# Group softmax: tiles of 256 rows with two adjacent rows per partition, on one queue

## The chip, the cores and the metric

One core of one Trainium2 chip runs the kernel. The metric is the device time of one execution in microseconds, the slowest core's, here the only one's.

## The reference

```python
def reference(x):                       # x: 4 x 4096 x 4352, float32
    x_g = x.reshape(B, N, 8, D // 8)    # 8 groups of 544 in a row
    x_g = x_g - x_g.max(axis=-1, keepdims=True)
    exp = np.exp(x_g)
    out = exp / exp.sum(axis=-1, keepdims=True)
    return out.reshape(B, N, D).astype(np.float32)
```

There are 16,384 rows of 17,408 bytes. Every byte is read once and written once: 285.2 MB each way.

## The kernel before

A tile is 128 rows, one per partition. Loads and stores go out on one queue. Per tile, VectorE (DVE) takes the eight maxima, ScalarE (ACT) does eight exponentials that also sum, and DVE does one reciprocal and eight scalings, in place.

```python
NBUF = 12
pool = ctx.enter_context(tc.tile_pool(name="io", bufs=NBUF))
xg = xf.rearrange("n (g d) -> n g d", g=G)
nt = N // P                                            # 128 tiles
def load(i):
    xt = pool.tile([P, G, Dg], f32, name="xt")         # 17 KB per partition
    nc.sync.dma_start(out=xt, in_=xg[i * P:(i + 1) * P])
# ... store, expo (max and 8 exponentials), scale (reciprocal and 8 scalings)
AHEAD = NBUF - 2
for i in range(AHEAD):
    load(i)
for i in range(nt + 1):
    if i < nt:
        expo(i)
    if i:
        scale(i - 1)
        store(i - 1, nc.sync)
        if i - 1 + AHEAD < nt:
            load(i - 1 + AHEAD)
```

## Time and profile before

| | before |
|---|---|
| time, median of the first 3 runs | 1342.13 us (1341.66 to 1342.44) |
| span of the profiled run | 1340.1 us |
| moved by the 16 DMA engines | 429 to 432 GB/s in mid kernel |
| DVE busy, ACT busy | 78%, 57% |
| store waits ahead of a load, in the queue | 116 waits, 1104.5 us |

Read it from the rate down. The rate is flat, no compute engine is full, and the queue spends its time waiting for stores to land before it reuses their buffers. The prediction shows the lines.

Two kinds of figure below come from the trace's own records and not from a line of a view. The first is the record of each packet on a DMA engine: start, duration, bytes. The second is the 16 landings of each transfer, one per DMA engine (before: 4,096 for 256 transfers). "Lag" means how much later the slowest engine lands its share of a transfer than the median engine. "Row" means one contiguous piece moved between memory and one partition, which is one packet (before: 32,768 packets of 17,408 B, and 4,096 of 4 B that end a transfer on an engine). "Steady" means the median engine's time for one transfer in mid kernel. A "ring" is the list of transfers that one DMA engine still has to do. SP is the engine whose sequencer (SPq in the views) issues the transfers of the queue.

### The profile page before, as it was taken

The page shows a single profiled execution, that of the slowest core. Times are in us where ns is not written, and L with a number is a line of the kernel's source. Part 1 is how long each engine was busy: PE and PEld are TensorE (multiplying, and loading weights), DVE is VectorE, ACT ScalarE, POOL GpSimd, SP SyncE. Part 2 cuts the span into 40 slices and gives each one's busy share as a digit, 9 for nine tenths or more (in the row PEclk, how much of TensorE's full clock was granted, in tenths as well). Part 3 has the DMA queues.
Part 4 walks back from the last instruction along what each step waited for, and adds up shares of the span by engine and source line. Part 5 has one row for each costly group of instructions (what it writes and reads, how often), then busy time and mean ns, then how long its engine had stood idle before and what let it go on. Part 6 is the DMA issues. An engine that isn't in the chain of part 4 may idle for free.

```text
span 1340.1 us, 4119 instructions
## 1 busy us (share of the span) xinstructions
DVE 1046.7 (78%) x1280; ACT 764.3 (57%) x2049; POOL 0.2 (0%) x4
## 2 busy tenths in 40 slices
DVE  6999987878777887888777877778877887777760
ACT  5777766555655565556555556555665556555540
POOL 0000000000000000000000000000000000000000
DMA  9999999999999999999999999999999999999996
GB/s 399 426 429 431 430 430 432 432 432 431 431 432 430 432 431 432 431 431 431 431 430 431 432 430 432 431 430 431 431 432 430 432 431 429 430 431 431 430 432 266
DMA packets 36896, 570.70 MB, mean 426 GB/s; under 512 B 4096, under 2 KB 4096, under 8 KB 4096
## 3 DMA queue, kind: packets, MB, share of 16 engines
q1 hardware_dynamic: 36864, 570.44, 99.4%
q14 instruction: 32, 0.26, 0.0%
HBM read 285.21 MB, written 285.21 MB: 426 GB/s over the span
## 4 chain that ended last, share of the span: by engine, by line
DMA 88%; DVE 7%; SPq 1%; ACT 1%; issue 1%; DVEq 0%; ACTq 0%
DMA out_dram<-xt 85%; DVE mx L45 4%; DVE xt L63 3%; DMA xt<-in_x_dram 3%; SPq L37 1%; ACT xt L49 1%; DVE rs L61 0%; DVEq L104 0%; ACTq L104 0%
## 5 line engine op out<-in xcount | busy, mean ns | idle before, releaser
L49 ACT ACTIVATE xt<-xt,mx 128x544 f32<-128x544 f32 x1024 | 751.2, 735 | 524.3 <-issue 435.8
L45 DVE TENSOR_REDUCE mx<-xt 128x8 f32<-128x4352 f32 x128 | 599.6, 4685 | 247.6 <-DMA xt<-in_x_dram 247.6
L63 DVE TENSOR_SCALAR xt<-xt,rs 128x544 f32<-128x544 f32 x1024 | 434.2, 498 | 4.5
L49 ACT ACTIVATION_READ_ACCUMULATOR xt<-xt,mx 128x1 f32 x1024 | 191.3, 187 | 0.0
L61 DVE RECIPROCAL rs<-sm 128x8 f32<-128x8 f32 x128 | 24.7, 193 | 3.4 <-ACT xt L49 3.4
L49 ACT ACT_TABLE_LOAD x1 | 1.3, 1283 | 9.9 <-DMA xt<-in_x_dram 9.9
L93 POOL MEMSET const-bfloat16-1.0<- 128x1 bf16 x1 | 0.1, 101 | 0.0
L93 POOL MEMSET const-uint8-127<- 128x1 uint8 x1 | 0.1, 101 | 0.0
L93 POOL MEMSET const-float32-0.0<- 128x1 f32 x1 | 0.1, 98 | 0.2 <-issue 0.2
L93 POOL MEMSET const-float32-1.0<- 128x1 f32 x1 | 0.1, 98 | 0.0
## 6 DMA issues: line engine op xcount, KB each, us to landing
xt<-in_x_dram SPq DMA_DIRECT2D x128, 2176.0 KB, 25.8
out_dram<-xt SPq DMA_DIRECT2D x128, 2176.0 KB, 30.6
```

Of the source, the lines that this page charges most:

```text
L37: nc.sync.dma_start(out=xt, in_=xg[i * P:(i + 1) * P])
L45: nc.vector.reduce_max(out=mx, in_=xt, axis=mybir.AxisListType.X, negate=True)
L49: nc.scalar.activation(out=xt[:, g, :], in_=xt[:, g, :], func=mybir.ActivationFunctionType.Exp, bias=mx[:, g:g + 1], scale=1.0, accum_out= ...
L61: nc.vector.reciprocal(out=rs, in_=sums.pop(i))
L63: nc.vector.tensor_scalar_mul(out=xt[:, g, :], in0=xt[:, g, :], scalar1=rs[:, g:g + 1])
L93: nc = _bacc.Bacc("TRN2", target_bir_lowering=False, num_devices=1)
```

## The change

The intent is fewer and longer transfers with the same buffer space: two adjacent rows per partition make one contiguous row of 34 KB, 128 transfers take the place of 256, and the queue alternates store i and load i+5. The kept core of the diff:

```diff
-    NBUF = 12
+    R = 2
+    NBUF = 6
...
+    def rows(dram, i):
+        at, r = spans[i]
+        return dram[at:at + r * P].rearrange("(p r) d -> p (r d)", r=r)
+
     def load(i):
-        xt = pool.tile([P, G, Dg], f32, name="xt")
+        xt = pool.tile([P, R * D], f32, name="xt")
         tiles[i] = xt
-        nc.sync.dma_start(out=xt, in_=xg[i * P:(i + 1) * P])
+        nc.sync.dma_start(out=xt[:, :spans[i][1] * D], in_=rows(xf, i))
...
-    AHEAD = NBUF - 2
+    AHEAD = NBUF - 1
+    work = [(i, r) for i in range(nt) for r in range(spans[i][1])]
...
+        for n in range(len(work) + 1):
+            if n < len(work):
+                expo(*work[n])
+            if n:
+                i, r = work[n - 1]
+                scale(i, r)
+                if r == spans[i][1] - 1:
+                    store(i)
+                    if i + AHEAD < nt:
+                        load(i + AHEAD)
```

`expo` and `scale` do to row r of tile i what they did to a tile, with the same instructions.

More of the change, by code (lines that the diff above doesn't have):

```diff
@@ L23, with store, row, expo @@
     Dg = D // G
-    xg = xf.rearrange("n (g d) -> n g d", g=G)
-    og = of.rearrange("n (g d) -> n g d", g=G)
-    nt = N // P
+    f32 = mybir.dt.float32
     pool = ctx.enter_context(tc.tile_pool(name="io", bufs=NBUF))
     small = ctx.enter_context(tc.tile_pool(name="small", bufs=4))
-    f32 = mybir.dt.float32
+    spans = []
+    at = 0
+    while at < N:
+        r = min(R, (N - at) // P)
+        spans.append((at, r))
+        at += r * P
+    nt = len(spans)
     tiles = {}
     sums = {}
+    def rows(dram, i):
+        at, r = spans[i]
+        return dram[at:at + r * P].rearrange("(p r) d -> p (r d)", r=r)
     def load(i):
-        xt = pool.tile([P, G, Dg], f32, name="xt")
+        xt = pool.tile([P, R * D], f32, name="xt")
         tiles[i] = xt
-        nc.sync.dma_start(out=xt, in_=xg[i * P:(i + 1) * P])
-    def store(i, eng):
-        eng.dma_start(out=og[i * P:(i + 1) * P], in_=tiles.pop(i))
-    def expo(i):
-        xt = tiles[i]
+        nc.sync.dma_start(out=xt[:, :spans[i][1] * D], in_=rows(xf, i))
+    def store(i):
+        nc.sync.dma_start(out=rows(of, i), in_=tiles[i][:, :spans[i][1] * D])
+    def row(i, r):
+        return tiles[i][:, r * D:(r + 1) * D].rearrange("p (g d) -> p g d", g=G)
+    def expo(i, r):
+        xr = row(i, r)
         mx = small.tile([P, G], f32, name="mx")
-        nc.vector.reduce_max(out=mx, in_=xt, axis=mybir.AxisListType.X, negate=True)
+        nc.vector.reduce_max(out=mx, in_=xr, axis=mybir.AxisListType.X, negate=True)
         sm = small.tile([P, G], f32, name="sm")
-        sums[i] = sm
+        sums[i, r] = sm
         for g in range(G):
             nc.scalar.activation(
-                out=xt[:, g, :],
-                in_=xt[:, g, :],
+                out=xr[:, g, :],
+                in_=xr[:, g, :],
                 func=mybir.ActivationFunctionType.Exp,
@@ L56, in expo, with scale @@
             )
-    def scale(i):
-        xt = tiles[i]
+    def scale(i, r):
+        xr = row(i, r)
         rs = small.tile([P, G], f32, name="rs")
-        nc.vector.reciprocal(out=rs, in_=sums.pop(i))
+        nc.vector.reciprocal(out=rs, in_=sums.pop((i, r)))
         for g in range(G):
-            nc.vector.tensor_scalar_mul(out=xt[:, g, :], in0=xt[:, g, :], scalar1=rs[:, g:g + 1])
-    AHEAD = NBUF - 2
+            nc.vector.tensor_scalar_mul(
+                out=xr[:, g, :], in0=xr[:, g, :], scalar1=rs[:, g:g + 1])
+    AHEAD = NBUF - 1
+    work = [(i, r) for i in range(nt) for r in range(spans[i][1])]
     with tc.manual_schedule():
@@ L70 @@
             load(i)
-        for i in range(nt + 1):
-            if i < nt:
-                expo(i)
-            if i:
-                scale(i - 1)
-                store(i - 1, nc.sync)
-                if i - 1 + AHEAD < nt:
-                    load(i - 1 + AHEAD)
+        for n in range(len(work) + 1):
[8 more added lines that the diff above has]
+                        load(i + AHEAD)
 _INS = ['x']
```

## The prediction

> **What bounds the kernel now.** I read the page first, for busy shares and the rate of the transfers.
>
> ```profile
> span 1340.1 us, 4119 instructions
> DVE 1046.7 (78%) x1280; ACT 764.3 (57%) x2049; POOL 0.2 (0%) x4
> ...
> GB/s 399 426 429 431 430 430 432 432 432 431 431 432 430 432 431 432 431 431 431 431 430 431 432 430 432 431 430 431 431 432 430 432 431 429 430 431 431 430 432 266
> ...
> q1 hardware_dynamic: 36864, 570.44, 99.4%
> HBM read 285.21 MB, written 285.21 MB: 426 GB/s over the span
> ```
>
> DVE and ACT have room; the 16 DMA engines are busy for 99.4% of the span and move 430 to 432 GB/s in every slice but the first two and the last. Then the queue's own waits and its timeline, to see what holds the queue back:
>
> ```profile
> SPq L37 <- DMA out_dram<-xt: 1104.5, 116, 16.7
> ```
>
> ```profile
> 105.00 0.33 SPq L37 DMA_DIRECT2D xt<-in_x_dram  x1
> 105.38 0.81 SPq L40 DMA_DIRECT2D out_dram<-xt  x1
> 115.38 0.33 SPq L37 DMA_DIRECT2D xt<-in_x_dram  x1
> 115.76 0.79 SPq L40 DMA_DIRECT2D out_dram<-xt  x1
> ```
>
> 116 loads wait for a store that has to free their buffer, and as soon as one goes out the next store follows 0.4 us later: the result was ready long before. One load and one store take 10.3 us, which is 4.456 MB at 431 GB/s. The chain of waits agrees, 85% of it stores and nothing else for a thousand us. DVE's 247.6 us of waiting for loads is the other face of it: compute runs up to the newest tile and then stands. Last, the tail, by stretches (columns: stretch, its us, busy us of DVE, ACT, POOL, clock, DMA share, GB/s):
>
> ```profile
> 1310.00:1320.00 10.00, 0.00 (x0) 0.00 (x0) 0.00 (x0) 1.00 1.00 428
> 1320.00:1325.00 5.00, 0.00 (x0) 0.00 (x0) 0.00 (x0) 1.00 0.97 414
> 1325.00:1330.00 5.00, 0.00 (x0) 0.00 (x0) 0.00 (x0) 1.00 0.24 101
> 1330.00:1335.00 5.00, 0.00 (x0) 0.00 (x0) 0.00 (x0) 1.00 0.19 80
> 1335.00:1340.10 5.10, 0.00 (x0) 0.00 (x0) 0.00 (x0) 1.00 0.08 34
> ```
>
> Twelve or thirteen DMA engines are through at about 1325.5 us. Three work on alone (0.19 of 16 is 3), the last until 1339.3. The landings of each store on the 16 engines show it building up: the slowest engine is 1.6 us behind the median at the first load, 6.2 us behind half way and 13.8 us at the end. So **the bound is the slowest DMA engine, which never stands idle**; everything else waits for it.
>
> [...]
> [...] In the tail, where single engines can be followed packet by packet, each row has a record of 648 ns and the next starts 644 to 645 ns after it[...]. The 4-byte packet that ends each transfer on an engine shifts the next by 6 ns (its record is 9 ns).
> [...] 12 tiles of 17 KiB and 6 of 34 KiB are both 204 KiB[...].
>
> **The change part by part.**
> (1) Descriptors. 256 transfers with 8 rows per engine become 128 with 8 rows of 34,816 B. [...] One engine before: 256 x (8 x 644.7 + 6 ns) = 1321.9 us; the undisturbed engines in fact take from 1.8 to 1325.5, 1323.7 us. After: 128 x (8 x 1284.7 + 6 ns) = 1316.3 us. Saved: **5.6 us**, 4.8 of it from 1024 rows fewer per engine at 4.7 ns and 0.8 from 128 end packets at 6 ns. It falls on the slowest engine too, so it is on the path in full.
> (2) The slow engines' lag. The trace has 32 instruction fetches of 8 KB on a queue of their own; each occupies one engine for about 309 ns, and the next row there has a record lengthened by 100 to 530 ns. DVE and ACT keep exactly the same instructions (1280 and 2049), only the queue's sequencer has 128 transfers fewer. So I leave the 13.8 us as they are, with some 3 us either way: change **0**.
> (3) Queue depth. Before, a load waits for the store three earlier; when it is released, two loads and two stores of 5.16 us are still in the rings, 20.6 us. After, load i+5 waits for store i-1, with load i+4 and store i behind it: 2 x 10.3, again 20.6 us. The lag of 14 us fits within that in both, so the fast engines do not run dry either, and the slowest certainly not. Change **0**.
> (4) Compute. Per two rows of each partition DVE has 2 x (4.69 + 0.19 + 3.39) = 16.5 us, ACT 2 x 5.9 = 11.8, against 20.6 us of transfer. The one new delay: the second row of tile i is scaled only after the first maximum of tile i+1, so store i can go some 4.7 + 3.6 = 8.3 us after load i+1 landed. It is wanted 31 us after that landing (store i-3, load i+2, store i-2 come between, at 10.3 each). Margin 22 us where it was about 48. Change **0**.
> (5) Ends. The first load lands about 5.2 us later (10.3 instead of 5.16 of transfer), so DVE starts at 15 instead of 9.9 and store 0 is ready at about 37 us. But five loads keep the rings full until about 54 us, as ten did. At the end the last load is followed by five stores, 51.6 us, as by ten before; the last tile needs about 4.7 + 2 x 5.9 + 4.7 = 22 us and its store is wanted after 41. Change **0**.
> Sum: 1342.1 - 5.6 = **1336.5 us**, 0.4% faster.
>
> **Rivals.**
> *Fixed cost is not per row.* If the long row is cut into pieces of the old size, or if the gap of 4.7 ns comes with bytes and not with rows, only the end packets go: 1342.1 - 0.8 = 1341.3. For it: before there is one row size only, so the trace cannot show the split by itself[...]. One chance in seven.
> *The rows of one tile get coupled.* If the order between instructions is kept for the whole tile and not for the row touched, the second maximum has to wait for the first row's exponentials, and the first scaling for the second row's. A tile then costs DVE 4.69 + 5.9 + 4.69 + 5.9 + 3.6 = 24.8 us, more than 20.6; 64 of them are 1587 us, and with ends about 1600, 19% slower. Nothing in the trace before can show it, since there a tile had one maximum and one scaling. The rows are separate column ranges, so I give it one chance in twenty or less.
> *A coarser pipeline starves.* Fewer, bigger pieces could leave the rings empty when something is late by over 20 us. The longest waits in the trace are 4.6 us (ACT, for nothing shown) and 9.9 (DVE, first load); margins of 20 and 22 us take them. If one in ten of the 64 turns lost 2 us, it would be 13 us more, 1349.
> *The lag changes.* [...] if the fetches spread differently, 3 us either way.
>
> **Range and chances.** Centre 1336.5. The cut-row rival and a lag larger by 3 us reach 1341; a lag smaller by 3 to 4 us, or rows with even less overhead, reach 1332. The runs before spread over 0.8 us only. Range 1332 to 1341.5. Over 2% faster would be below 1315[...]: 0.01. Over 2% slower needs the coupling or a real starvation: 0.05. Within 2%: 0.94.
>
> **What will show it.** Packets about 18,432 on the queue, with 16,384 rows; a row's record near 1288 ns, and 1285 from start to start. The rate in mid slices at 433 instead of 431. Loads waiting for stores on the queue still, about 58 of them, and one load plus one store every 20.57 us. Tail: most engines done near 1320, the last some 13 us later. DVE and ACT busy times unchanged. Wrong would be: rows still of 648 ns; the queue waiting for DVE's scaling in mid kernel; ACT or DVE waiting for each other within a tile at each turn; a slice below 425 GB/s.

Passages are cut where marked; no term of the sum is: 1342.1 - 5.6 = 1336.5 us, with 1284.7 ns for the long row and 4.7 ns for each row fewer. Before the change, with one row size, the trace gave only the 644.7 ns from start to start (mean of 112 on the engine that ends last; 650 to 651 across an end packet, so 6 ns for it), and the other two were the assumption. The records after have 1284.7 ns there (mean of 105), and 2 x 644.7 - 1284.7 is 4.7 ns.

## The result, and the profile after

| | before | after |
|---|---|---|
| time, median of 4 runs | 1342.04 us | 1335.57 us (1334.61 to 1336.10) |
| span of the profiled run | 1340.1 us | 1333.5 us |
| ratio | | 0.9951, 95% interval 0.9934 to 0.9968 |

Ratios here and below are the mean time of one kernel's runs over that of the other's of the same rounds, so they are not quite the ratio of the medians quoted. Executions over 1.5% slower than the fastest of the same kernel are left out of the means. The kernel is faster, clear of noise, by half a per cent; at the 2% threshold it is the same.

The page after has the lines that answer to those of before:

```profile
span 1333.5 us, 3809 instructions
DVE 1041.7 (78%) x1280; ACT 764.4 (57%) x2049; POOL 0.2 (0%) x4
...
GB/s 403 428 423 432 432 432 431 433 432 431 432 432 434 434 432 434 430 434 434 434 431 433 434 434 434 431 432 435 432 434 432 431 434 434 433 435 433 433 433 283
...
q1 hardware_dynamic: 18432, 570.43, 99.3%
q14 instruction: 28, 0.23, 0.0%
```

The packets have halved to 18,432. DVE and ACT do the same work. The rate in mid kernel is some 2 GB/s higher, but the third slice is not: 423 in place of 429.

The queue's own waits and two turns of its timeline (start, duration, instruction):

```profile
SPq L47 <- DMA out_dram<-xt: 1145.0, 58, 20.7
SPq L50 <- DVE xt L76: 91.2, 7, 22.5
```

```profile
87.39 0.33 SPq L47 DMA_DIRECT2D xt<-in_x_dram  x1
87.81 0.38 SPq L50 DMA_DIRECT2D out_dram<-xt  x1
108.66 0.33 SPq L47 DMA_DIRECT2D xt<-in_x_dram  x1
109.04 0.42 SPq L50 DMA_DIRECT2D out_dram<-xt  x1
```

The wait is the same one: 58 loads, each for a store that frees its buffer, with the next store ready 0.4 us later. Of the seven waits for the scaling, four (40.1 us) lie before 200 us, where compute catches up, and three (51.1 us) after 1250 us, at the last stores; none lies between. The DMA share is 0.97 or more in every stretch from 5 to 1320 us, so they cost next to nothing. The tail by stretches (us, busy us of DVE, ACT and POOL, clock, DMA share, GB/s):

```profile
1310.00:1320.00 10.00, 0.00 (x0) 0.00 (x0) 0.00 (x0) 1.00 0.98 425
1320.00:1325.00 5.00, 0.00 (x0) 0.00 (x0) 0.00 (x0) 1.00 0.29 125
1325.00:1330.00 5.00, 0.00 (x0) 0.00 (x0) 0.00 (x0) 1.00 0.13 56
1330.00:1333.50 3.50, 0.00 (x0) 0.00 (x0) 0.00 (x0) 1.00 0.05 20
```

Most engines finish just after 1320 us. Two (0.13 of 16 is 2) work on to 1332. So the end still belongs to the slowest DMA engine.

The 6.6 us between the two profiled spans split up as follows.

| | before | after | difference |
|---|---|---|---|
| 256 rows loaded and stored, steady | 20.652 us | 20.563 us | -0.089 us; 64 times: -5.7 us |
| last landing, median engine | 1325.4 us | 1320.9 us | -4.5 us |
| lag of the slowest engine at the last store | 13.9 us | 11.7 us | -2.2 us |

The steady rate gains 5.7 us, the start gives 1.1 us of it back, and a smaller lag adds 2.2 us. The start is visible in the stretches of 40 to 60 and 60 to 100 us, first before, then after:

```profile
40.00:60.00 20.00, 19.93 (x23) 14.86 (x41) 0.00 (x0) 1.00 1.01 425
60.00:100.00 40.00, 39.82 (x51) 29.81 (x80) 0.00 (x0) 1.00 1.00 430
```

```profile
40.00:60.00 20.00, 19.89 (x29) 14.84 (x40) 0.00 (x0) 1.00 0.99 409
60.00:100.00 40.00, 39.82 (x50) 29.16 (x81) 0.00 (x0) 1.00 1.00 427
```

409 in place of 425 GB/s for 20 us is 0.8 us, 427 in place of 430 for 40 us is 0.3 us. Such stretches count whole rows, so their edges are rough, but the landings agree: how far they run ahead of those before, followed back from mid kernel to the start along a straight line, gives 1.05 us lost here and 0.6 us in the repetition below. The DMA share is 0.99, so no ring is empty there; the last two rows of the fifth load, just ahead of the first store, are longer, and this load lands 11.1 us after the fourth in place of 10.3. Rows starting between 50 and 60 us carry 13.4 us above their normal length after (28 of them by over 20 ns), 5.0 us before (17). Why they are longer was not tried.

### The profile page after: what moved, and what is told of

It is laid out like the page before. It is cut to its first block, busy times and chain, and to the rows that moved or that the text cites. A ratio compares the mean times of both kernels' runs of the same rounds, so it can differ in the third digit from the quotient of the medians.

```text
span 1333.5 us, 3809 instructions
## 1 busy us (share of the span) xinstructions
DVE 1041.7 (78%) x1280; ACT 764.4 (57%) x2049; POOL 0.2 (0%) x4
## 4 chain that ended last, share of the span: by engine, by line
DMA 92%; DVE 4%; ACT 1%; SPq 1%; issue 0%; DVEq 0%; ACTq 0%
DMA out_dram<-xt 89%; DMA xt<-in_x_dram 3%; DVE mx L58 2%; DVE xt L76 1%; ACT xt L62 1%; SPq L47 1%; DVE rs L74 0%; DVEq L121 0%; ACTq L121 0%; ACTq L62 0%; SPq L50 0%
```

## The experiments

Theory A is the prediction's: each DMA engine pays a fixed cost of about 4.7 ns per row and 6 ns for the packet that ends a transfer, whatever the length, and the slowest engine sets the end. (From start to start in the last transfers, 17,408 B took 644.7 ns before and 34,816 B took 1284.7 after: two short rows cost 4.7 ns more than a long one. The end packet shifts the next row by 6 ns in both.) Rival B: the gain is from the number of transfers, the queue's turns or their order. Rival C: it is a smaller lag, by luck. Eleven kernels were run. The first four ran together on one chip, the next four together, and the last three together, each with its own runs of the kernel before (medians 1342.10, 1342.49 and 1341.54 us; single runs from 1339.59 to 1343.53).

### The change again

The edit is none.

> The changed kernel once more, beside the three others on one chip. Theory A (a fixed cost of about 4.7 ns per row and 6 ns per end packet on every DMA engine) and every rival: 1335.6 us within 1 us, ratio 0.995. It gives the noise of the lag: if the last DMA engine's lag differs by more than 2 us from the 11.7 us of the first run, part of the 6.5 us is luck.

Measured: 1336.38 us (1335.29 to 1336.96), ratio 0.9960 (0.9947 to 0.9972). Steady: 10,282.3 ns for a transfer, 10,281.5 the first time. Lag at the end: 12.9 us, where it was 11.7. The steady part repeats to a nanosecond; the lag differs by a microsecond between the two profiles, and the times of single runs by up to 2.4 us.

### The same transfers with rows of 17 KB

```diff
-        return dram[at:at + r * P].rearrange("(p r) d -> p (r d)", r=r)
+        return dram[at:at + r * P].rearrange("(r p) d -> p r d", r=r)
```

(The tile side of both transfers is viewed as `p r d` to match.)

> The changed kernel with its tiles, its buffers, its queue order and its 128 transfers, but with row p and row p+128 in partition p, so that each transfer has 256 rows of 17 KB again. Theory A: 1024 more rows per engine at 4.7 ns, 4.8 us, give 1340.4 us (ratio to before 0.9988), packet records of 648 ns. Rival B (the gain is from the halved number of transfers, end packets and queue turns, or from the new queue order): 1335.6 us. Rival C (the gain is a smaller lag by luck): either.

Measured: 1339.09 us (1338.35 to 1339.27), ratio 0.9979 (0.9967 to 0.9992). The page has twice the data packets:

```profile
q1 hardware_dynamic: 34816, 570.43, 99.6%
```

Its time lies between the two theories' numbers, so the total alone does not decide. The landings do. Steady, a transfer takes 10,320.3 ns here and 10,282.3 with long rows: 38 ns, times 128 is 4.9 us, against 4.8 expected by theory A and 0 by B. Against the kernel before (2 x 5,163.0 ns) it is 5.7 ns per transfer less: the one end packet that is saved, predicted as 6. So both terms of the sum hold, and **the row length is what the steady gain comes from**. What moves the total off 1340.4 is the lag: 11.4 us in this profile, 12.9 us in the one above, 13.9 us in the profile before.

### Rows of 52 KB

```diff
-    R = 2
-    NBUF = 6
+    R = 3
+    NBUF = 4
```

> The changed kernel with three adjacent rows per partition, four buffers and 86 transfers: rows of 52 KB. Theory A: 336 rows fewer per engine at 4.7 ns and 42 end packets fewer at 6 ns, 1.8 us less than the changed kernel: 1333.8 us, packet records near 1928 ns. Rival (a coarser pipeline starves): store i is now ready 8 us after load i+1 landed, and the rings have about 31 us of work behind a freed buffer, so no loss is expected in mid kernel, but if a margin is missed it is 1340 us or more and the queue waits for the scaling. Rival (long rows are cut): records of at most 34 KB lengths and 1335 to 1340 us.

Measured: 1336.49 us (1335.99 to 1337.77), ratio 0.9962 (0.9950 to 0.9975). The expected 1.8 us did not come. The rows are not cut: 10,752 packets of 52,224 B with records of 1,928 ns, and steadily 15,404.7 ns for a transfer, where theory A has 8 x 1924.7 + 6 = 15,403.6 (1284.7 ns and another 640.0 for 17,408 B more). The rings ran dry at the start:

```profile
40.00:60.00 20.00, 19.93 (x26) 15.61 (x43) 0.00 (x0) 1.00 0.87 376
60.00:100.00 40.00, 39.83 (x51) 29.18 (x79) 0.00 (x0) 1.00 1.01 417
```

In the queue's timeline load 3 goes out at 50.21 us, behind store 0, while its buffer was free from the beginning and the three first loads (46 us of transfer) are through. So my check of the margins had covered mid kernel and not the start.

### Rows of 52 KB, all four buffers loaded at the start

```diff
-        for i in range(AHEAD):
+        for i in range(NBUF):
             load(i)
...
-                    if i + AHEAD < nt:
+                    if NBUF <= i + AHEAD < nt:
```

> The kernel of e3_rows52 with its fourth buffer loaded at the start, where e3 issued load 3 only behind store 0, at 50.2 us, when the first three loads were nearly through; e3 moved 376 GB/s between 40 and 60 us. Theory (rows of 52 KB cost 1.8 us less per engine than rows of 34 KB, and e3 lost some 4 us of that and more to rings that ran dry in its first 100 us): 1332 to 1333 us. Rival (the long rows themselves bring nothing more): 1336 us as the changed kernel, with no gap at 40 to 60 us.

Measured: 1333.49 us (1333.20 to 1334.45), ratio 0.9944 (0.9931 to 0.9958). The stretch of 40 to 60 us of this kernel:

```profile
40.00:60.00 20.00, 19.93 (x26) 15.60 (x43) 0.00 (x0) 1.00 0.98 423
```

One extra load at the start is worth about 3 us (2.4 by the ratios, each to its own kernel before), and it uncovers the gain of the longer rows, which in the steady part is 17.6 ns for 384 rows loaded or stored, 1.5 us over the run. Its median is 2.9 us under that of the changed kernel and 2.1 us under the first measurement. It was run at another time. It beats the kernel before; that it beats the changed kernel too is not shown, since the two ratios' intervals overlap.

### Rows cut into pieces of 2,176 B

```diff
-        xt = pool.tile([P, G, Dg], f32, name="xt")
+        xt = pool.tile([P, G, Dg + 4], f32, name="xt")[:, :, :Dg]
```

> The kernel before with 16 unused bytes behind each group in the tile, so that each row of 17 KB becomes 8 pieces of 2,176 B; same tiles, transfers, order and compute. Theory A: 14,336 more pieces per engine (256 transfers x 56) at 4.7 ns, 67 us: 1409 us, ratio 1.050, starts of pieces about 84.7 ns apart. If the gap came with bytes and not with pieces: 1342 us.[...]

Measured: 1444.45 us (1444.37 to 1444.48), ratio 1.0766. A miss: the direction and the kind are right, but theory A's 67 us are 102. Steady, a transfer takes 5,583.2 ns, so a piece takes 87.1 ns and not 84.7. In the last transfer the starts are these:

```
start to start, ns:  85  90  84  90  84  90  85  89  85  89
```

The mean of 87.1 is two values in turn. One is the 84.7 ns of theory A, the other, 89 to 90 ns, about 5 ns more. So in this store every second piece, of equal length, is slower; why was not shown. At the start, where only loads run, a transfer takes 5,650 to 5,760 ns, which theory A does not cover either. The next run tests whether the excess goes away.

### Rows cut into pieces of 4,352 B

```diff
-        xt = pool.tile([P, G, Dg], f32, name="xt")
+        xt = pool.tile([P, 4, D // 4 + 4], f32, name="xt")[:, :, :D // 4]
```

(The views of the tile in transfers and compute follow.)

> The kernel before with 16 unused bytes behind every second group in the tile, so that each row of 17 KB becomes 4 pieces of 4,352 B[...]. Theory A (about 4.7 ns per piece[...]): 6,144 more pieces per engine, 28.9 us, 1371 us, ratio 1.0215, starts 164.7 ns apart. Rival (a piece costs 7.1 ns, as the mean of e4_rows2 says[...]): the extra pieces at 7.1 and the old rows at 2.4 more, 48 us, 1390 us.

Measured: 1371.74 us (1370.60 to 1374.19), ratio 1.0220 (1.0205 to 1.0236), as theory A had it, and starts 164 to 165 ns apart. These pieces cost 4.8 ns each, and the turns of 85 and 90 ns are gone. What made every second piece of 2,176 B slower is not shown by that, because the size of the piece and the places where pieces start changed together.

A rival for both totals is the issuing of the transfers. In both kernels the queue was busy issuing nearly throughout: one issue mostly took 5.0 to 5.8 us, where it took 0.3 to 0.8 before. Against it speaks the end of the run with 2,176 B: the last issue was over at 1427.7 us, and the last transfer, after 1436 us, still has starts 84 to 90 ns apart, 87 on average.

All sizes side by side, one transfer on one engine, steady, in ns. The estimate is from the starts in the last transfers before and after: 644.7 ns for 17,408 B and 1284.7 for 34,816 give bytes at 27.2 B/ns and 4.7 ns per piece, and the end packet has its 6 ns. So the rows of these two kernels test it least:

| kernel | pieces per engine | estimate | measured | fixed cost per piece |
|---|---|---|---|---|
| 2,176 B | 64 | 5,427 | 5,583.2 | 7.1 |
| 4,352 B | 32 | 5,276 | 5,279.1 | 4.8 |
| 17,408 B, before | 8 | 5,164 | 5,163.0 | 4.6 |
| 17,408 B, 256-row transfers | 16 | 10,321 | 10,320.3 | 4.6 |
| 34,816 B, after | 8 | 10,284 | 10,281.5 | 4.4 |
| 52,224 B | 8 | 15,404 | 15,404.7 | 4.8 |

### A shallower ring in the kernel before

```diff
-    AHEAD = NBUF - 2
+    AHEAD = NBUF - 1
```

> The kernel before with its lookahead raised from NBUF-2 to NBUF-1: a load now waits for the last but one store and finds 10.3 us of work in the rings in place of 20.6. Theory (the slowest DMA engine sets the end, and it is the one whose store is waited for, so it never runs dry): 1342 us as before, but the fast engines run dry once the lag passes 10.3 us, so the last landing of the slowest engine is at most about 10.5 us after the median. Rival (the queue order and depth are part of what the change gained or could lose): a difference of 2 us or more either way.

Measured: 1371.40 us as the median of four runs (1356.69 to 1378.99; the slowest of these is left out of the ratio), ratio 1.0179 (1.0115 to 1.0243), which is 24 us. Whether that reaches 2% is unclear; that it is slower is not. A clear miss. The lag did come out smaller, 5.9 us at the end, but the time did not stay. Two stretches of the profiled run, first a good one, then a bad one:

```profile
200.00:560.00 360.00, 285.07 (x350) 205.73 (x553) 0.00 (x0) 1.00 1.01 431
590.00:740.00 150.00, 108.36 (x135) 81.92 (x221) 0.00 (x0) 1.00 1.00 397
```

Until about 560 us it runs as before. Then, with the lag at 6.7 us and rising to 10.0, the rate falls, and again from 1050 to 1250 us, with lags of 7 to 8. The DMA share stays 1.00, so the engines are not idle in the view: single rows get longer, one in a hundred takes over 1.18 us in place of 0.65. Over the run 1,421 rows are longer by over 20 ns, 515 us together, 32 us per engine, which is the loss: the median engine's last landing is 33 us later than before, and the smaller lag gives 8 us back. In the profile before there are 171 such rows and 42 us. So with 10.3 us of work behind a freed buffer in place of 20.6 this pattern loses about 2%, and the theory that the slowest engine alone matters, whatever the others do, is too simple. What stretches the rows stays open.

### A deeper ring in the changed kernel

```diff
-    AHEAD = NBUF - 1
+    AHEAD = NBUF - 2
```

> The changed kernel with its lookahead cut from NBUF-1 to NBUF-2, as the kernel before had it: load i+4 waits for store i-2, with 31 us of work in the rings behind it in place of 20.6. e6_ahead11 showed that 10.3 us are too few (1371 us). Theory (20.6 us cover the lag of 12 us, so more depth brings nothing): 1336 us within 1 us. Rival (the changed kernel still loses to a shallow queue): up to 3 us less.

Measured: 1336.30 us (1335.81 to 1339.86), ratio 0.9969 (0.9955 to 0.9982). Three of four runs lie within 1335.8 to 1336.4. More depth brings nothing; 20.6 us, which both kernels of the change have, is enough. The fourth run, the profiled one, had a lag of 15.9 us and lost time in the tail. Its instructions are those of the changed kernel, so the lag of one and the same work came out at 11.7, 12.9 and 15.9 us in three profiles.

### Half of ACT's instructions (a wrong result on purpose)

```diff
+            if g % 2:
+                continue
             nc.scalar.activation(
-                out=xr[:, g, :],
-                in_=xr[:, g, :],
+                out=xr[:, g:g + 2, :],
+                in_=xr[:, g:g + 2, :],
```

(Reciprocal and scaling use the four sums; sums and bias are those of a pair, so the result is wrong by 0.5 in relative error.)

> The changed kernel with ACT working on pairs of groups: 512 ACTIVATE of 1088 columns in place of 1024 of 544, and half the accumulator reads. The result is wrong on purpose (sums and bias of a pair are shared). ACT then has 1024 instructions fewer, so some 8 of the 28 instruction fetches go. Theory L (the lag of the two slowest DMA engines is the fetches; one engine carries ACT's, about 17 to 19, the other DVE's, about 11): the lag of one engine falls to about 6 us, the other stays at 11 to 13, so the time stays within 1.5 us of 1336. Rival (the lag has nothing to do with fetches): both engines stay at 11 to 13.

Measured: 1335.15 us (1333.55 to 1339.30), ratio 0.9950. In the tail of the profile one engine alone is late, by 12.0 us, where two were; the other's lag fell to 5.6 us. The time did not move.

### One DVE multiplication for eight (a right result)

```diff
-        for g in range(G):
-            nc.vector.tensor_scalar_mul(
-                out=xr[:, g, :], in0=xr[:, g, :], scalar1=rs[:, g:g + 1])
+        nc.vector.tensor_tensor(
+            out=xr, in0=xr, in1=rs.unsqueeze(2).to_broadcast([P, G, Dg]), op=mybir.AluOpType.mult)
```

> The changed kernel with DVE's eight scalings of a row as one multiplication with the reciprocals repeated (a right result), ACT as it was. 896 DVE instructions and some 7 fetches fewer. The theory of the fetches: one engine's lag falls to about 5 us, the one that carries ACT's stays at 12 to 13 us, the time stays within 1 us of 1336. If DVE's fetches were what counts: 1331 us.

Measured: 1336.67 us (1334.21 to 1338.63), ratio 0.9965. Again one engine is late alone, by 12.3 us, and the next only by 4.2 us. The time did not move.

### Both at once (a wrong result on purpose)

The edit is the two above together.

> The same with DVE's eight scalings of a row replaced by one multiplication with the reciprocals repeated, 896 DVE instructions fewer; wrong on purpose in the same way. DVE's row is then expected at 4.7 + 0.2 + 4.6 us, 19 of the 20.6 us of a turn. Theory L: some 15 of the 28 fetches go, both lags fall to about 5 to 6 us and the end comes 6 us earlier, about 1330 us. Rival (lag not from fetches): 1336 us, lag 11 to 13 us. If DVE becomes the bound instead: the queue waits for the scaling in mid kernel and the time rises.

Measured: 1330.81 us (1329.31 to 1332.86), ratio 0.9913 (0.9897 to 0.9930); the lag is 7.6 and 4.6 us. DVE is busy for 4.692 us in the multiplication and still has time. The instruction queue's line of the page, for the changed kernel again, ACT halved, one multiplication, and both, in four fences:

```profile
q14 instruction: 28, 0.23, 0.0%
```

```profile
q14 instruction: 21, 0.17, 0.0%
```

```profile
q14 instruction: 22, 0.18, 0.0%
```

```profile
q14 instruction: 14, 0.11, 0.0%
```

The four runs are a square. Each half alone lowers one engine's lag and no time, both together lower both lags and the time by about 5 us. The two with ACT halved: the intervals of their ratios do not overlap (0.9933 to 0.9968 alone, 0.9897 to 0.9930 with the one multiplication). Following each engine by the joins of its packets (one starts where the last one ends) tells why. In the changed kernel two engines end last, at 1331.9 and 1332.2 us, and these two carry 17 and 10 of the 28 fetches of 8 KB, at intervals of some 75 and 124 us; the one that is left falls on a third engine. With ACT halved the counts are 9 and 10, with the one multiplication 17 and 3, with both 9 and 3, and one or two on a third. The landings show it step by step: the lag of the engine with 10 fetches stands still between them, and at the fetches at 426, 550, 675, 799, 923, 1048 and 1175 us it goes to 6.4, 7.3, 8.2, 9.1, 10.0, 10.9 and 11.8 us. So **the two late engines are late because they bring ACT's and DVE's instructions**, some 0.6 us per fetch on ACT's engine and 0.9 us on DVE's. The packets' records say the same: 309 ns for the fetch, and in most cases 260 to 370 ns more on the one engine and 540 to 620 ns more on the other for the row behind it. Not all of the lag is this: engines without a fetch end up to 4.2 us behind.

## Why the prediction was right

**The bound** was named rightly: DMA, and in it the slowest engine's chain. The one addition is from the shallow ring: the slowest engine is the end only while the rings are deep enough. Three lines were read a little off, without effect on the sum: the slices before run from 429 and not from 430 GB/s, half way the lag was 7.1 us and not 6.2, and ACT's longest wait behind DVE's maximum was 5.4 us.

**Part 1, descriptors**, predicted 5.6 us: the steady rate gained 5.7. Its two terms were seen apart: 4.9 us for the rows (predicted 4.8) and 5.7 ns for the end packet (predicted 6). The rival that the cost comes with bytes or that long rows are cut is out: records of 1,288 ns, starts 1,284.7 apart, and the same 4.4 to 4.8 ns from 4 KB to 52 KB.

**Part 2, the lag**, predicted as unchanged within 3 us: it fell from 13.9 to 11.7 us in the first profile and to 12.9 in the second. This is inside the allowance, but it is part of the 6.6 us between the two profiles, and with lags of 11.7 to 15.9 us for the same work it counts as luck. Four instruction fetches fewer (28 in the span in place of 32) can be a part of it: before, the counts were 18 and 11, and 3 on the third engine. At 0.6 and 0.9 us each, one fewer on each late engine gives an estimate of at most 0.9 us at the end; no run tested that. The statement that the instructions of DVE and ACT set the lag is shown by the square of four.

**Part 3, depth**, predicted 0: a deeper ring gains nothing. That the depth does matter below that, 24 us at 10.3, I had not expected.

**Part 4, compute**, predicted 0: the waits show no coupling of the rows of a tile. DVE waited for ACT only 4.0 us in all, so the rival of 1587 us is out. The same view has ACT waiting 504 us, 119 times, for DVE's maximum, which looks like a sign of error that I had named; but before, ACT stood idle as long (77.9 us put down to DVE, 435.8 us to nothing shown), and the queue waited for no scaling in mid kernel:

```profile
DVE rs L74 <- ACT xt L62: 4.0, 2, 2.6
```

**Part 5, ends**, predicted 0: store 0 went out at 36.16 us, predicted about 37, and the rings stayed full, but the start cost 1.1 us through longer rows just ahead of the first store. The sign of error that I had named, a slice under 425 GB/s, is there once between the first slice and the last, the third with 423. This loss and the smaller lag partly cancel, which is why 1336.5 lies within a microsecond of 1335.57; the sum is partly lucky, its main term is not.

## What to carry to other kernels

When the DMA engines are full from end to end, a longer row wins only what each piece costs, here 4.4 to 4.8 ns from 4,352 B up: work out pieces times 4.7 ns before you rebuild tiles. Here it was under half a per cent between 17 and 34 KB, 2% at 4,352 B and 8% at 2,176 B, where 35 of the 102 us are the excess over theory A that the pieces of 4,352 B did not have. Keep well more work in the rings than the slowest engine lags (20.6 us were enough for lags of 12 to 14; 10.3 us were not for lags of 7 to 10), and load every free buffer at the start. Then look at the tail: if a few DMA engines end late, count the instructions of every engine, since fetching them takes DMA time (here 309 ns for 8 KB, and 0.6 or 0.9 us of lag each), and all the late ones must be relieved before the time moves.
